# Eight adaptive rows as matrix products of a broadcast column with raw weight tiles, in a three-layer transformer kernel

## The chip, the cores and the metric

The kernel runs on one core of one Trainium2 chip. The metric is the device time of one execution in microseconds (us), the median of several runs. The engines are named as in the profile: PE (TensorE, with PEld for its weight loads), DVE (VectorE), ACT (ScalarE), POOL (GpSimd) and SP (SyncE, whose queue issues most loads). Each engine works through its own instructions in the order in which they stand.

## The reference, cut to what matters

The program is a hybrid layer (attention with a learned choice of keys, a short convolution, a mixture of 64 experts) and two more transformer layers behind it, on 512 tokens of 1024 features. The change touches one vector of the first layer:

```python
ada = jax.nn.silu(c) @ w_ada + b_ada            # [1, 6 * 1024]
shift1, scale1, gate1, shift2, scale2, gate2 = [a[:, None, :] for a in jnp.split(ada, 6, axis=-1)]
h = rms_norm(x, norm1_g) * (1 + scale1) + shift1
proj = h @ w_in                                  # conv inputs, q, k, v, index q, index k, index weights
score = relu(qi . ki) weighted by wi             # the 128 best keys of each query are kept
x = x + gate1 * mix
h2 = rms_norm(x, norm2_g) * (1 + scale2) + shift2
x = x + gate2 * moe(h2, ...)
```

`w_ada` is 1024 x 6144, 24 MB in float32. Its 6144 columns are handled in twelve groups of 512, numbered 0 to 11. Groups 2, 0, 3 and 1 (scale1 and shift1) are needed before the first projection; the other eight, in the order 8, 9, 6, 7, 4, 5, 10, 11, are needed only after attention. They are the "late rows".

## The kernel before, in words

Each matrix product is made from two exact parts of both operands (`split`, L217 on ACT and L218 on DVE or POOL, makes them; `mm3`, L225 to L227, makes three products). Weights come through `_Stream`: SP loads 1 MB raw tiles (`wraw`) ahead, in the order of `plan_attn`, and the tiles of `w_ada` are used raw. All eight PSUM banks belong to one pool (`ps()`), and most large SBUF tiles to another.

`attn_block` does, in this order on PE: the early ada rows and the normalised, transposed tokens (until 62.5 us); the second half of the index queries (`first(wb, ...)`, four chunks of 12 products); the index keys (`psk`, 24 products); then `proj` for k, for q and for v. Each `proj` holds four accumulators, one per token tile `tt`, and goes through eight chunks `kc` of 12 products (four token tiles by three). After each chunk `tick()` emits one step of each piece of background work: `heads_T` (normalises k or q on DVE, L478 to L492 and the rotation L420 to L423, transposes on PE, L230, and splits, L220 and L221), `topk` (index scores on PE, L725 on ACT and L728 to L737 on DVE, then 16 rounds of L748 and L752 on DVE, ending in the mask `selbias`, L756) and `aw`, the late rows. Twenty steps of the convolution follow, then attention, whose first product of each query tile reads `selbias` (L816).

A late row has four steps of `aw`. In a step ACT scales two 128 x 512 slices of the raw tile by a column of silu(c) (L655) and POOL adds them up (L657). Two rows later `ada_sum` makes one product of a matrix of ones with the sum (L605), which adds over the partitions and puts the result on all of them, and DVE adds it to the row (L608, L609 or L611). `ada_feed`, called where `proj` takes a weight tile, takes the two raw tiles of the next row and issues the loads of bias and gain on ACT's queue when its count reaches NR, NR + 1 and NF.

The early rows (`ada`, L545) are already made in the other way: `cb` holds silu(c) with each value repeated along 128 columns, and eight float32 products of `cb` with a raw slice give the row on all partitions.

Of the kernel before, what the change touches and what calls it, by code (L numbers as in the profile page):

```python
# [23 lines left out]
NT = 4  # L24
# [9 lines left out]
# slots of an expert by its rank: those below the first number have the second  # L34
# [3 lines left out]
NR=3; RQ=3; RV=2  # L38
NF=7
BU=1  # L40
ADA='aaaaaaaa'
# [29 lines left out]
class _Stream:  # L71
    """Weights in the order of use: loads run ahead on the SP queue, and each tile is split into two
    parts of at most 12 significant bits, whose sum is the float32 value, before it is used."""
# [57 lines left out]
    def more(self):  # L131
        """prepare one more tile than `ahead` asks for"""
        if self.ns < len(self.jobs):
            if self.ns not in self.rawt:
                self.pump(self.ns)
            self._split()
            self.pump(self.ns)
# [40 lines left out]
class _K:  # L178
# [53 lines left out]
    def rsqrt(self, v, n, scale, eps, name):  # L232
        """1 / sqrt(scale v + eps): a seed from the exponent, a third-order step and a Newton step, each on a
        multiple of the result that spares a product"""
# [42 lines left out]
    def tick(self):  # L277
        """emit one step of each piece of background work"""
        self.todo[:] = [g for g in self.todo if next(g, self) is not self]
# [5 lines left out]
    def proj(self, hT, nk, tiles, n=512, hook=None, w=None):  # L285
        """token-major product: weight tiles [p, kk, n] from chunk kc0 on into four PSUM tiles"""
# [14 lines left out]
    def by_tile(self, part, done, early=()):  # L301
        """products that end tile by tile: done(tt, *part(tt)) goes on by a step once the next tile's products
        are emitted; the functions `early` come after the last tile's products, a step of `done` apart"""
# [16 lines left out]
    def part(self, hT, ps, tt, ws):  # L320
        """token tile tt of a product, weight tiles [(first chunk, tile)]"""
# [7 lines left out]
    def begin(self, xT):  # L329
        """the products of a block's first two weight tiles [128, 8, 256] with the first half of the tokens"""  # L330
# [16 lines left out]
    def begun(self, xT):  # L347
        """what `begin` has left of the next of its weight tiles"""
        w, ps = self.head.pop(0)
        self.cols(xT, w, ps, slice(256, 512))  # L350
        return ps

    def chunks(self, name, n):
        """feature-major operand in chunks of 128 features by 512 columns, as its two exact parts"""
# [58 lines left out]
    def rope_p(self, t, cc, ss):  # L413
        """rotate the first 16 of each 64 columns of t [128, G, 64]; cc [128,16], ss [128,16] = [-sin | sin]"""
# [50 lines left out]
    def row(self, dst, ap, off, n):  # L465
        """one DRAM row on all partitions"""
        self.nc.scalar.dma_start(out=dst, in_=bass.AP(tensor=ap.tensor, offset=ap.offset + off, ap=[[0, 128], [1, n]]))

    def heads_T(self, dst, ps, g=None, scale=None):
        """four PSUM tiles [128 tok, 8 x 64]: (RMS norm with gain g,) partial rotation, feature-major split;  # L470
        the gain of the rotated columns goes in before the rotation, that of the others, in `scale`, after it"""
# [33 lines left out]
    def attn_block(self):  # L505
        nc, V, a, st = self.nc, self.nc.vector, self.a, self.st
        # adaptive scale and shift, and the normalised tokens, by halves of the features
# [86 lines left out]
        # remaining adaptive rows, on the scalar and Pool engines  # L594
# [4 lines left out]
        wait = []  # L599

        def ada_sum():
            n, t = wait.pop(0)
            ps = self.ps()
            c = slice((n % 4) * 512, (n % 4) * 512 + 512)
            nc.tensor.matmul(ps, ones, t, start=True, stop=True)  # L605
# [22 lines left out]
        def ada_work():  # L628
            for i, n in enumerate(todo):
                while not fed:  # L630
                    yield
                ws = fed.pop(0)
                if len(wait) > 1:
                    ada_sum()
                t = self.sm([128, 512], "p", bufs=3)
                col = lambda j, kk: cs[:, 4 * j + kk:4 * j + kk + 1]
                if ADA[i] == "d":
                    for j in range(2):
                        for kk in range(4):
                            x, c = ws[j][:, kk], col(j, kk)  # L640
                            if j + kk:
                                V.scalar_tensor_tensor(t, x, c, t, op0=OP.mult, op1=OP.add)
                            else:
                                V.tensor_scalar(t, x, c, None, OP.mult)
                            if kk % 2:
                                yield
                else:
                    ts = self.slot(F32, "adap")
                    for j in range(2):
                        for kk in range(4):  # L650
                            x = ts[:, kk * 512:kk * 512 + 512]
                            if ADA[i] == "p" or ADA[i] == "h" and kk % 2:
                                nc.gpsimd.tensor_scalar(x, ws[j][:, kk], col(j, kk), None, OP.mult)
                            else:
                                nc.scalar.activation(x, ws[j][:, kk], AF.Copy, scale=col(j, kk))  # L655
                            if j + kk:
                                nc.gpsimd.tensor_tensor(out=t, in0=x if j or kk > 1 else ts[:, :512], in1=t if j or kk > 1 else x, op=OP.add)  # L657
                            if kk % 2:
                                yield
                wait.append((n, t))  # L660
            yield self
        aw = ada_work()
        # indexer queries, keys, weights
# [43 lines left out]
        # indexer scores  # L707
# [31 lines left out]
        def topk():  # L739
            """the 128 best keys of each query, the earlier of equal ones: others get a bias of -1e30"""  # L740
# [23 lines left out]
        # values  # L764
# [5 lines left out]
        # short convolution, channel-major  # L770
# [34 lines left out]
        while wait:  # L805
            ada_sum()
        # attention
# [41 lines left out]
        # the rest of the output projection and the residual, then the normalised tokens of the expert half  # L849
# [29 lines left out]
    def out_head(self, mix, add):  # L879
        """the first four chunks' share of an output projection; add(tt, ps, n) takes it in"""  # L880
# [22 lines left out]
    def pipeline(self, items, stages, fill=None, n=0, ready=None):  # L903
        """stages [(fn, delay)] over items; each step also emits up to n units of the background work `fill`,
        and as much of it as an item needs to be ready"""
# [24 lines left out]
    def attend(self, heads, logits, value, fill=None, n=0, bufs=3, ready=None):  # L930
        """softmax attention of `heads` in tiles of 128 queries, feature-major result"""
# [34 lines left out]
    def moe_units(self):  # L966
        """(ranks, rows of the slot blocks), in the order of work: the first FIX experts; the others by falling
        number of tokens, the busiest with two blocks, the least busy two to a block"""
# [50 lines left out]
    def moe_begin(self, hT):  # L1019
        """the router and most of the shared expert's first products, on the first half of the tokens"""  # L1020
# [66 lines left out]
    def moe_block(self, hT, h2d, x1d):  # L1087
# [20 lines left out]
        pos_b = self.const.tile([128, NT, NE], BF16, name="pos_b")  # exact up to 256, and above stays above  # L1108
# [10 lines left out]
        def pack(v, g, tmp):  # L1119
            """the gate in three exact parts"""  # L1120
# [8 lines left out]
        def tables(c, ig, is_):  # L1129
            """gather and scatter rows of n blocks from the sums c [128, n, 3] of token, tile base and one"""  # L1130
# [1015 lines left out]
```

## Time and profile before

| what | value |
|---|---|
| median of three runs | 2726.62 us |
| lowest and highest of them | 2722.79 and 2729.9 us |
| span of the profiled execution | 2724.9 us |
| mean granted clock of PE in it | 0.938 of full speed |
| PE busy in the span | 2361.5 us, 87% |
| DVE, ACT, POOL busy | 1649.5, 1056.4, 836.8 us |

The profile gives no time of that execution apart from its span, so the span stands for both; it lies 1.7 us under the median. Averages over the span say little about the change, which touches only the stretch from 62 to 260 us.

### The profile page before, as it was taken

What the parts mean: (1) busy time and instruction counts of PE and PEld (TensorE: products, weight loads), DVE (VectorE), ACT (ScalarE), POOL (GpSimd) and SP (SyncE); (2) the same over time, 40 slices, a digit from 0 to 9 for tenths busy, and PEclk for the clock granted to TensorE, in tenths of its full rate; (3) what the DMA queues carried; (4) which work ended last, traced back from release to release, by engine and by line L of the source; (5) the groups of instructions that cost most, each with busy time, mean ns of one, the idle gap of its engine ahead of it and who ended that gap; (6) DMA issues with size and microseconds to landing.
All of it is one profiled execution on the core that took longest, in us unless ns stands there. A gap on an engine that the chain in (4) does not pass through costs nothing.

```text
span 2724.9 us, 33197 instructions
## 1 busy us (share of the span) xinstructions
PE 2361.5 (87%) x12964; PEld 1979.8 (73%) x12964; DVE 1649.5 (61%) x2445; ACT 1056.4 (39%) x1446; POOL 836.8 (31%) x308
## 2 busy tenths in 40 slices
PE   8778996778777887888758998999999998899998
PEld 4556765677666776777757877888888886788887
DVE  4699666577877877677656655333354666533234
ACT  2642433355545655555542532221313443222221
POOL 0653243456645655565521120000032221100001
PEclk9889998899988988898979999999999998999999
DMA  9432145588967877888861042223232122222321
GB/s 317 171 122 63 47 157 188 192 264 273 308 212 245 287 260 248 278 278 279 271 182 45 16 152 88 85 93 108 87 114 70 47 72 81 95 89 81 123 70 39
DMA packets 176593, 422.40 MB, mean 155 GB/s; under 512 B 19281, under 2 KB 97873, under 8 KB 151729
## 3 DMA queue, kind: packets, MB, share of 16 engines
q1 hardware_dynamic: 151552, 353.43, 37.8%
q0 software_dynamic: 12944, 39.20, 6.7%
q10 hardware_dynamic: 11938, 27.62, 2.8%
q8 instruction: 103, 1.69, 0.2%
q14 instruction: 56, 0.46, 0.1%
HBM read 390.78 MB, written 35.52 MB: 156 GB/s over the span
## 4 chain that ended last, share of the span: by engine, by line
PE 50%; DVE 22%; issue 9%; DMA 7%; ACT 6%; POOL 6%; ACTq 0%; POOLq 0%; DVEq 0%; SPq 0%
PE b L225 16%; PE b L226 15%; PE b L227 15%; DVE wl L218 5%; POOL wl L218 4%; ACT wh L217 4%; DMA acc<-eo,isc 3%; PE b L230 2%; DMA wraw<-in_w_dram 2%; DVE xet L218 1%; DVE gt L1140 1%; DVE work L752 1%; DVE eo L1414 1%; PE b L545 1%; POOL acc L1218 1%
## 5 line engine op out<-in xcount | busy, mean ns | idle before, releaser
L218 POOL TENSOR_TENSOR wl<-wraw,wh 128x2048 fp32r<-128x2048 f32 (+2 forms) x113 | 533.0, 4720 | 1208.6 <-ACT wh L217 1157.8
L218 DVE TENSOR_TENSOR wl<-wraw,wh 128x2048 fp32r<-128x2048 f32 x198 | 606.9, 3072 | 367.8 <-ACT wh L217 319.6
L217 ACT ACTIVATE wh<-wraw 128x2048 fp32r<-128x2048 f32 (+2 forms) x311 | 583.5, 1884 | 151.3 <-DVE wl L218 58.0
L225 PE MATMUL b<-xtl,wh 128*128 128x512 f32 (+1 forms) x928 | 342.5, 369 | 2.9 <-DVE xtl L218 2.9
L226 PE MATMUL b<-xth,wl 128*128 128x512 f32 (+1 forms) x928 | 341.0, 368 | 4.0 <-POOL wl L218 4.0
L227 PE MATMUL b<-xth,wh 128*128 128x512 f32 (+1 forms) x928 | 340.7, 367 | 0.0
L225 PE MATMUL b<-wl,xet 128*128 128x256 f32 x1072 | 319.2, 298 | 0.1
L226 PE MATMUL b<-wh,xet 128*128 128x256 f32 x1072 | 311.3, 290 | 0.8 <-DVE xet L218 0.8
L227 PE MATMUL b<-wh,xet 128*128 128x256 f32 x1072 | 310.8, 290 | 0.0
L1218 POOL DMA_INDIRECT acc<-eo,isc x67 | 102.6, 1531 | 391.9 <-DVE P L1152 121.6
L225 PEld LDWEIGHTS b<-wl,xet 128*128 128x128 f32 x1072 | 214.7, 200 | 1.7 <-ACT xet L217 0.2
L226 PEld LDWEIGHTS b<-wh,xet 128*128 128x128 f32 x1072 | 214.0, 200 | 2.4 <-DVE xet L218 0.9
L227 PEld LDWEIGHTS b<-wh,xet 128*128 128x128 f32 x1072 | 213.2, 199 | 0.0
L225 PE MATMUL b<-wl,aet 128*128 128x512 f32 x268 | 125.5, 468 | 99.6 <-POOL wl L218 99.1
L226 PEld LDWEIGHTS b<-xth,wl 128*128 128x128 f32 x928 | 175.0, 189 | 32.8 <-POOL wl L218 4.6
L225 PEld LDWEIGHTS b<-xtl,wh 128*128 128x128 f32 x928 | 175.0, 189 | 32.3 <-DVE xtl L218 3.6
L227 PEld LDWEIGHTS b<-xth,wh 128*128 128x128 f32 x928 | 174.9, 189 | 28.9
L225 PEld LDWEIGHTS b<-wl,aet 128*128 128x128 f32 x268 | 57.8, 216 | 121.2 <-POOL wl L218 108.8
L225 PE MATMUL b<-wl,ath 128*128 128x512 f32 x352 | 137.1, 390 | 0.0
L227 PE MATMUL b<-wh,ath 128*128 128x512 f32 x352 | 136.9, 389 | 0.0
L226 PE MATMUL b<-wh,atl 128*128 128x512 f32 x352 | 136.9, 389 | 0.0
L1213 POOL DMA_INDIRECT xg<-h2d,ig x51 | 124.6, 2444 | 34.3 <-issue 17.5
(463 smaller groups left out, 4649.8 us busy)
## 6 DMA issues: line engine op xcount, KB each, us to landing
wraw<-in_w_dram SPq DMA_DIRECT2D x192, 1024.0 KB
wraw<-in_ffn_w_gu_dram SPq DMA_DIRECT2D x44, 1024.0 KB
wraw<-in_w_ada_dram SPq DMA_DIRECT2D x24, 1024.0 KB
wraw<-in_ffn_w_down_dram SPq DMA_DIRECT2D x20, 1024.0 KB
wraw<-in_diff_w_in_dram SPq DMA_DIRECT2D x12, 1024.0 KB
wraw<-in_w_in_dram SPq DMA_DIRECT2D x8, 1024.0 KB
wraw<-in_w_in_dram SPq DMA_DIRECT2D x12, 512.0 KB
x<-in_x_dram SPq DMA_DIRECT2D x8, 512.0 KB
```

The lines of the kernel that those rows point to most:

```text
L217: nc.scalar.activation(H, x, AF.Copy)
L218: (eng or nc.vector).tensor_tensor(out=L, in0=x, in1=H.bitcast(F32), op=OP.subtract)
L225: mm(ps, s[0], m[1], start=start, stop=False)
L226: mm(ps, s[1], m[0], start=False, stop=False)
L227: mm(ps, s[0], m[0], start=False, stop=stop)
L230: self.nc.tensor.transpose(ps, x, self.ident[:x.shape[0], :x.shape[0]])
L545: nc.tensor.matmul(ps, cb[:, kc, :], w[:, kk, :], start=False, stop=kc == 7)
L752: V.match_replace(work(qt), m8[qt - 1], work(qt), -3e38)
L1140: V.tensor_tensor(out=gt, in0=c[:, :, 2], in1=c[:, :, 1], op=OP.add)
L1213: nc.gpsimd.indirect_dma_start(out=x, out_offset=None, in_=h2d, in_offset=IndirectOffsetOnAxis(ap=idx, axis=0), bounds_check=S - 1, oob_is ...
L1218: nc.gpsimd.indirect_dma_start(out=acc, out_offset=IndirectOffsetOnAxis(ap=idx, axis=0), in_=o, in_offset=None, compute_op=OP.add)
L1414: V.tensor_scalar(o[rows, c], ps[rows], gate[rows], None, OP.mult)
```

## The change

The late rows are made as the early ones are. A step of `aw` is now two float32 products on PE, `cb` with two raw slices, summed in a PSUM bank that the row holds through its four steps. `ada_sum`, the ACT scalings, the POOL sums, their tiles `adap` and `p` and the products with ones are gone. The DVE sum with the bias (`ada_row`) stands right after the row's last step and no longer two rows later. NR goes from 3 to 1, so that the loads of gain and bias are issued with the first and second row. (Comments and docstrings are gone too.)

```diff
-NR=3; RQ=3; RV=2
+NR=1; RQ=3; RV=2
...
-        wait = []
-
-        def ada_sum():
-            n, t = wait.pop(0)
-            ps = self.ps()
+        def ada_row(n, ps):
             c = slice((n % 4) * 512, (n % 4) * 512 + 512)
-            nc.tensor.matmul(ps, ones, t, start=True, stop=True)
             r = rows[(n - 4) // 4][:, c]
...
         def ada_work():
-            for i, n in enumerate(todo):
+            for n in todo:
                 while not fed:
                     yield
                 ws = fed.pop(0)
-                if len(wait) > 1:
-                    ada_sum()
-                t = self.sm([128, 512], "p", bufs=3)
-                col = lambda j, kk: cs[:, 4 * j + kk:4 * j + kk + 1]
...
-                    ts = self.slot(F32, "adap")
-                    for j in range(2):
-                        for kk in range(4):
-                            x = ts[:, kk * 512:kk * 512 + 512]
...
-                                nc.scalar.activation(x, ws[j][:, kk], AF.Copy, scale=col(j, kk))
-                            if j + kk:
-                                nc.gpsimd.tensor_tensor(out=t, in0=x if j or kk > 1 else ts[:, :512], in1=t if j or kk > 1 else x, op=OP.add)
-                            if kk % 2:
-                                yield
-                wait.append((n, t))
+                ps = self.ps()
+                for j in range(2):
+                    for kk in range(4):
+                        kc = 4 * j + kk
+                        nc.tensor.matmul(ps, cb[:, kc, :], ws[j][:, kk, :], start=kc == 0, stop=kc == 7)
+                        if kk % 2:
+                            yield
+                ada_row(n, ps)
...
         self.drain()
-        while wait:
-            ada_sum()
```

On PE, at the head of the projection for q, these rows stood before: the product with ones (out of `p`), then the first chunk's products of three of the four token tiles, with the engines that each waits for.

```order
L605 MATMUL b<-p,ones_f 128x512 [waits Activation_49,Pool_49]
L225 MATMUL b<-wl,hth 128x512 [waits Activation_49]
L226 MATMUL b<-wh,htl 128x512
L227 MATMUL b<-wh,hth 128x512
...
L225 MATMUL b<-wl,hth 128x512 [waits DVE_49]
L226 MATMUL b<-wh,htl 128x512
```

In the changed kernel (its line numbers are lower by one or more) the same place reads so; `g_98` is the tile that holds `cb`, and L633 is the new product.

```order
L633 MATMUL b<-wraw,g_98 128x512 [waits DMAHW4_49,Activation_49]
L633 MATMUL b<-wraw,g_98 128x512
L224 MATMUL b<-wl,hth 128x512 [waits Activation_49]
...
L224 MATMUL b<-wl,hth 128x512 [waits DVE_49]
L225 MATMUL b<-wh,htl 128x512
L226 MATMUL b<-wh,hth 128x512
L224 MATMUL b<-wl,hth 128x512 [waits DVE_49,Activation_49]
L225 MATMUL b<-wh,htl 128x512
L226 MATMUL b<-wh,hth 128x512
L633 MATMUL b<-wraw,g_98 128x512 x2
L224 MATMUL b<-wl,hth 128x512
```

A pair of new products now stands ahead of every chunk of k, q and v, and two token tiles of the first chunk wait for DVE where one did. The built program gives the fourth token tile of q the bank of k's first accumulator, so its wait is for the DVE multiply that reads that accumulator last (L490, L489 in the changed kernel); before, it had the bank of the ones product and waited for the row's sum (L611). At the head of v it is the same with q's first accumulator.

On DVE, at the start of the stretch, these rows stood before: the split of the index-key weights, those of both tiles of k's weights, and the first row's sum and gain.

```order
L218 TENSOR_TENSOR wl<-wraw,wh 128x576
L218 TENSOR_TENSOR wl<-wraw,wh 128x2048 x2
L608 SCALAR_TENSOR_TENSOR row_417<-b,row_417 128x512
L609 TENSOR_TENSOR row_417<-row_417 128x512
L420 TENSOR_TENSOR rpa_590<-t2k,rope_c 128x128
```

Now they stand so:

```order
L217 TENSOR_TENSOR wl<-wraw,wh 128x576
L603 SCALAR_TENSOR_TENSOR row_417<-b,row_417 128x512
L604 TENSOR_TENSOR row_417<-row_417 128x512
L217 TENSOR_TENSOR wl<-wraw,wh 128x2048
L603 SCALAR_TENSOR_TENSOR row_417<-b,row_417 128x512
```

The sums of the first two rows moved ahead of the splits of k's two weight tiles.

## Rows read from the trace of the kernel before

**Rows 1.** The page's first line, the whole execution.

```profile
span 2724.9 us, 33197 instructions
```

**Rows 2.** Windows: stretch, length, busy time of PE, PEld, DVE, ACT, POOL; clock.

```profile
62.50:126.90 64.40, 53.35 (x223) 38.48 (x221) 37.96 (x79) 35.78 (x56) 41.41 (x28) 0.87 0.48 165
126.90:141.80 14.90, 11.31 (x40) 8.16 (x38) 14.16 (x20) 8.91 (x15) 8.45 (x6) 0.89 0.61 210
141.80:172.90 31.10, 24.39 (x126) 18.41 (x127) 27.53 (x45) 15.87 (x29) 16.29 (x10) 0.89 0.20 68
172.90:191.80 18.90, 8.21 (x23) 5.98 (x24) 18.07 (x34) 8.34 (x14) 11.14 (x7) 0.64 0.63 195
191.80:256.90 65.10, 53.38 (x230) 41.56 (x228) 64.55 (x171) 17.41 (x22) 25.36 (x12) 0.97 0.33 82
```

**Rows 3.** Waits of PE, 62.5 to 257 us: total, times, longest.

```profile
PE b L225 <- DVE row L611: 19.0, 3, 10.7
PE b L230 <- DVE t2k L700: 5.4, 4, 3.9
PE b L225 <- ACT t2k L679: 2.7, 1, 2.7
PE b L225 <- ACT t2k L495: 2.5, 1, 2.5
```

**Rows 4.** Chain that ended last: eight raw products, then one split product; start, us.

```profile
48.53 7.06 PE b L545 x16
55.83 0.23 PE b L226
```

**Rows 5.** Instructions of the tile adap, its readers among them: duration min/median/max.

```profile
L655 ACT ACTIVATE adap<-wraw,cs x64: 703/712/775, 66.3 to 217.2; 128x512 f32<-128x512 f32 x64
L657 POOL TENSOR_TENSOR p<-adap,p x48: 1262/1294/3225, 69.1 to 220.3; 128x512 f32<-128x512 f32 x48
```

**Rows 6.** Instructions of L492, L730 and L736 on DVE: min/median/max in ns.

```profile
L492 DVE TENSOR_TENSOR t2k<-t2k,q_norm_g x4: 292/554/4317, 191.8 to 211.2; 128x128 f32<-128x128 f32 x4
L730 DVE SCALAR_TENSOR_TENSOR work<-t2k,kwt,work x21: 484/750/1652, 123.1 to 175.3; 128x512 f32<-128x512 f32 x7, 128x384 f32<-128x384 f32 x7, 128x256 f32<-128x256 f32 x7
L736 DVE TENSOR_SCALAR work<-work x3: 417/1323/4628, 157.4 to 175.9; 128x512 f32<-128x512 f32 x1, 128x384 f32<-128x384 f32 x1, 128x256 f32<-128x256 f32 x1
```

**Rows 7.** Timeline of DVE, and one row of POOL: start, us, engine.

```profile
135.93 1.24 DVE L237 TENSOR_SCALAR rs_t<-hn_ss 128x32 f32<-128x32 f32 x1
141.12 0.69 DVE L490 TENSOR_TENSOR t2k<-b,hn_r 128x512 f32<-128x512 f32 x1
149.63 4.55 POOL L218 TENSOR_TENSOR wl<-wraw,wh 128x2048 fp32r<-128x2048 f32 x1 [1.67 <-ACT wh L217]
150.00 4.33 DVE L492 TENSOR_TENSOR t2k<-t2k,k_norm_g 128x128 f32<-128x128 f32 x1
189.10 0.18 DVE L237 TENSOR_SCALAR rs_t<-hn_ss 128x32 f32<-128x32 f32 x1
191.11 0.69 DVE L490 TENSOR_TENSOR t2k<-b,hn_r 128x512 f32<-128x512 f32 x1
256.53 0.90 DVE L756 TENSOR_SCALAR selbias<-work 128x256 fp32r<-128x256 f32 x3
257.94 1.28 DVE L611 TENSOR_TENSOR row<-row,b 128x512 f32<-128x512 f32 x2
```

**Rows 8.** Timeline of PE at the seams: start, us, idle before and releaser.

```profile
60.90 1.91 PE L230 MATMUL b<-ident,x 128*128 128x128 f32 x16
126.61 0.40 PE L227 MATMUL b<-kit,qith 64*128 64x512 f32 x2
133.58 0.74 PE L225 MATMUL b<-wl,hth 128*128 128x512 f32 x1 [3.31 <-DVE row L611]
172.44 0.28 PE L227 MATMUL b<-kit,qith 64*128 64x256 f32 x2
186.75 0.79 PE L225 MATMUL b<-wl,hth 128*128 128x512 f32 x1 [10.66 <-DVE row L611]
```

More of the change, by code (lines that the diff above doesn't have):

```diff
@@ L37 @@
 MORE=(5,6)
-NR=3; RQ=3; RV=2
+NR=1; RQ=3; RV=2
 NF=7
 BU=1
-ADA='aaaaaaaa'
 TC=3; TY=(1, 0, 0)
@@ L632, in ada_work @@
                 ws = fed.pop(0)
-                if len(wait) > 1:
-                    ada_sum()
-                t = self.sm([128, 512], "p", bufs=3)
-                col = lambda j, kk: cs[:, 4 * j + kk:4 * j + kk + 1]
-                if ADA[i] == "d":
-                    for j in range(2):
-                        for kk in range(4):
-                            x, c = ws[j][:, kk], col(j, kk)
-                            if j + kk:
-                                V.scalar_tensor_tensor(t, x, c, t, op0=OP.mult, op1=OP.add)
-                            else:
-                                V.tensor_scalar(t, x, c, None, OP.mult)
-                            if kk % 2:
-                                yield
-                else:
-                    ts = self.slot(F32, "adap")
-                    for j in range(2):
-                        for kk in range(4):
-                            x = ts[:, kk * 512:kk * 512 + 512]
-                            if ADA[i] == "p" or ADA[i] == "h" and kk % 2:
-                                nc.gpsimd.tensor_scalar(x, ws[j][:, kk], col(j, kk), None, OP.mult)
-                            else:
-                                nc.scalar.activation(x, ws[j][:, kk], AF.Copy, scale=col(j, kk))
-                            if j + kk:
-                                nc.gpsimd.tensor_tensor(out=t, in0=x if j or kk > 1 else ts[:, :512], in1=t if j or kk > 1 else x, op=OP.add)
-                            if kk % 2:
-                                yield
-                wait.append((n, t))
+                ps = self.ps()
[6 more added lines that the diff above has]
+                ada_row(n, ps)
             yield self
```

## The prediction, made before the changed kernel ran

> **What bounds the kernel now.** I read the page first: one execution spans 2724.9 us [rows 1], 1.7 under the median 2726.6, so the sum is made against the span and 1.7 is added at the end. The late rows lie between the last early transposes (PE, to 62.5) and the mask of the first attention tile (DVE, from 256.5, ready about 0.3 later). The windows of that stretch [rows 2] show who is full where. Until 126.9 PE is busy for 53.4 of 64.4 us; after that DVE is full (14.2 of 14.9, 27.5 of 31.1, 18.1 of 18.9, 64.6 of 65.1) and PE stands idle for parts. Over all five windows PE is busy 150.6 of 194.4 us, so 43.8 us are free, and its clock is below full. The waits [rows 3] say what PE waits for: 19.0 us for DVE row sums (L611), which stand behind DVE's index scores and rounds, 5.4 for index keys (L700), 5.2 for ACT copies that free banks (L679 and L495). So the stretch is a DVE chain that PE feeds: the scores of PE start DVE's rounds, and the normalisation on DVE gives PE back its banks.
>
> **The change, part by part.**
>
> *Price.* Eight raw products took 7.06 us at full clock, 0.88 each; a split product takes 0.23 [rows 4]. A pair costs 1.765. There are 32 pairs: 56.5 us on PE. The eight products with ones (the same shape, 0.88 each) go: 7.0. Net 49.4 us more PE work, against 43.8 us of idle time in the stretch. Off ACT go 64 x 0.712 = 45.6 us, off POOL 56 x about 1.29 = 72 us [rows 5]. Neither engine is the one waited for at the end of a window, so this counts only where it held DVE or PE. I put it in below.
>
> *A, 62.5 to the last index scores of 512 keys (126.9).* PE does 168 split products of 0.23 (48 index queries, 24 index keys, 96 for k), 38.6 us, score products 2.8, transposes 2.5 (my counts, each 0.45 per four) and two ones products 1.8: 45.7 us of work in 64.4. The rest is waiting and half clock. The waits for L679, L495 and L700 [rows 3] go away: ACT is free when the bank is to be emptied, and the DVE chain for the index keys starts earlier against a slower PE. 16 pairs come in: 45.7 - 1.8 + 28.2 = 72.1, so this point comes at 134.6, **+7.7**. The loads of gain and bias, now issued near 67 us, have 10 us before row 8 is done; I cost them at nothing. If they were late, k's splits on DVE would be too, with 10 us in hand.
>
> *B, from there to DVE's first L490 of k.* Before, 126.9 to 141.8. The chain from L237 to L490 took 5.2 us (135.93 to 141.12), and the same chain for q 2.0 (189.10 to 191.11), when POOL had no sums to make [rows 7]. So 3.2 us go: 11.7, which ends at 146.3, **+4.5** against before. Here is the new wait. The fourth token tile of q's first chunk used to wait for the row sum (L611, until 133.58 [rows 8]); it now waits for this L490, as its bank is k's first accumulator, the new row having taken a bank for four chunks. Queued behind it on PE is all the rest of q. PE, done with what it can do at 138.5, stands for 8 us.
>
> *C, from there to the last scores (before, 172.6 [rows 8]).* PE has 3 + 84 split products, 20.0 us, seven pairs, 12.4, scores and transposes, 5.3, and starts at half clock (before, after such a wait, the window's clock was 0.64 [rows 2] and PE lost half of some 3 us): 1.6. The split of v's first weight tile on POOL starts 2 us after the second k tile is back, as before, and then the two-input DVE instruction L492 took 4.33 instead of 0.29 us, to the end of POOL's 4.55 us [rows 6, 7]; this holds the row sum and so the scores by 3.5. Sum 42.8, to 189.1, **+16.5**. This is where most of the work lands: before, PE came to this point with 11 us of waits.
>
> *D, from the last scores to DVE's first L490 of q.* Before, 172.6 to 191.1 plus 0.7: 19.2. L736 was held by a POOL split, 4.63 us where its shortest is 0.42 [rows 6], so 4.2; the last seven L730 ran near the median of 0.750 where the minimum is 0.484, 1.9 [rows 6]; and the instruction behind L736 was held by most of one POOL sum of 1.29 [rows 5], 0.9. That is 7.0. In the changed order DVE reaches L736 about 1 us before POOL's split starts. 19.2 - 7.0 = 12.2, to 201.3, **+9.5** against 191.8. PE waits for it with v's fourth token tile; before, it waited only for the row sum (186.75 [rows 8]).
>
> *E, from there to selbias (256.5).* Before 64.7 us, all DVE. POOL's sums held three instructions, each by at most one of 1.29 [rows 5], 2.5 in all: these go. One more row sum falls in: +0.7. DVE has to wait for q's transposes, since a chunk on PE now takes 4.5 instead of 2.7 us: the first is back 12 us after the seam, and DVE has 9 us of work ahead of it, the later ones cost 1 more; +4.3. The convolution's first split on POOL still holds L492 (4.3 us, in the 64.7 already). 64.7 - 2.5 + 0.7 + 4.3 = 67.2, to 268.5, **+12.0**. PE alone would be there sooner: three products, 84 more, seven pairs, 1.8 of transposes, 27.3 for 120 convolution products, 1.6 of clock: 63 us.
>
> *After it.* The two row sums at 257.94 (1.28 us [rows 7]), ahead of attention's first reductions on DVE, are gone: **-1.3**. Nothing else moves; SP's loads stand in the same order, and the raw tiles of the last row are asked for when the last scores are done and used four chunks (18 us) later, so they cost nothing. I take the shift as carried to the end one to one, since the order behind it is unchanged.
>
> **Sum:** 12.0 - 1.3 = +10.7, 2735.6 on the span, **2737** on the median. The bounds of the unknown: the two POOL holds (in C and E) turn on tenths of a microsecond between ACT's split and DVE's L492. Without them C and E lose 3.5 and 4.0: +3.3, 2730. With a third (L736 in D, as before) it is +15, 2742.
>
> **A rule weighed against this.** The row for L492 shows 0.29 us alone and 4.33 beside a POOL split that ends when it ends [rows 6, 7]. The Trainium skill, GPSIMD Engine Reference, section "8. Key points", says that GpSimd shares its SBUF interfaces with VectorE and that they contend where the VectorE instruction has two SBUF inputs or a two-port mode; the trace agrees. By it every POOL sum taken away gives DVE time back, which speaks for the first rival.
>
> **Rivals.**
>
> 1. *Faster: DVE sets the end throughout, and PE's work fills its idle time.* DVE gets back what the POOL sums held: 3.2 in B, up to 21 x (0.750 - 0.484) = 5.6 in L730 [rows 6, 7], the 1.3 at the end, and 4.2 at L736: -14, **2712**. For it: DVE is full after 126.9 [rows 2], and 43.8 us of PE idle time nearly hold the 49.4. Against it: the idle time is idle because PE waits for DVE, and DVE's scores start when PE's products allow. It wins if the last scores come before 177, which needs PE to lose under 5 us in A to C. Chance 0.13.
>
> 2. *No change.* The same sum without the POOL holds, 2730, or with the shift partly absorbed by a later wait for weights or a scatter: **2730**. For it: the holds are a matter of tenths. Chance 0.40.
>
> 3. *Much slower: the bank held by the row stops PE at both seams, and little of the idle time is used.* If half of the 43.8 us stays idle, 49.4 - 21.9 = +27.5, less 3.2: **2751**. It decides if PE stands over 12 us at each seam. Chance 0.12.
>
> The forecast, slower by the sum above, 2733 to 2743, has 0.35.
>
> **How the numbers follow.** A measurement of this kernel tells about 0.3%, 8.2 us, from no change: 2718.4 to 2734.8 is the same. Faster is rival 1, 0.13. The same is rival 2 and a little of the forecast's low end, 0.43. Slower is the rest of the forecast and rival 3, 0.44. The range for 8 in 10 goes from inside rival 1 to rival 3: 2715 to 2750.
>
> **What would show it.** In the changed profile: 64 new raw products of L633 near 0.88 us, no wait for L679 or L700, the last 512-key score near 134.6, a PE wait of 7 to 9 us for the multiply L489 near 139 to 146 and one of about 10 us before 201, the last scores near 189, selbias near 268. ACT and POOL should be less busy by 46 and 72 us. The prediction is wrong if selbias comes before 256 (rival 1), if L492 is never held (rival 2), or if the stretch behind 268 does not keep the shift.

## The result, and the profile after

The changed kernel takes 2751.06 us (median), the kernel before, on the same chip, 2728.26: **1.0087 times as long, 95% interval 1.0073 to 1.0101**, or 22.8 us more. The forecast was slower by 10.7. The direction was right; the size was less than half of it, and 2751.06 lies 1.1 us above the range of 2715 to 2750.

The first lines of the changed kernel's page give the span and the busy time of each engine.

```profile
span 2750.2 us, 33232 instructions
PE 2411.0 (88%) x13076; PEld 2002.0 (73%) x13076; DVE 1622.5 (59%) x2445; ACT 1016.3 (37%) x1382; POOL 755.4 (27%) x252
```

PE is 49.5 us busier (its line of the page before has 2361.5), where the prediction had 49.4. This count also holds products that ran at half speed, so that it agrees so closely is in part luck; but the price of a pair, read below, was right too, and is not what went wrong. The windows of the changed kernel, cut at the same five events as [rows 2] (the end of the early transposes, the last 512-key scores, the first multiply of k, the last scores, the first multiply of q, the selection mask), show where the time went. The columns are those of [rows 2].

```profile
65.20:140.40 75.20, 74.40 (x280) 47.75 (x280) 29.18 (x82) 16.48 (x24) 0.00 (x0) 1.00 0.45 158
140.40:150.80 10.40, 4.08 (x14) 2.34 (x13) 9.81 (x20) 4.39 (x7) 0.00 (x0) 0.92 0.51 177
150.80:201.70 50.90, 46.66 (x180) 30.61 (x180) 22.37 (x45) 10.40 (x20) 4.57 (x1) 0.88 0.19 62
201.70:214.10 12.40, 5.01 (x14) 2.62 (x13) 11.76 (x32) 4.13 (x6) 4.54 (x1) 0.72 0.95 286
214.10:282.20 68.10, 64.83 (x262) 48.10 (x262) 63.16 (x171) 11.27 (x12) 13.81 (x3) 0.98 0.32 80
```

The lengths add up to 217.0 us; those of [rows 2] to 194.4. The difference, 22.6, is nearly the 22.8 that was timed; from the mask to the end both profiles take 2468.4 us. (The early transposes stand at 60.9 in the profile before and at 63.3 in this one. They lie between 58.3 and 63.3 in the profiles of all kernels here, whatever was edited, so stretches are counted from there on. The part behind the mask takes 2462 to 2479 us in these profiles, one execution of each kernel, so single microseconds of it can't be read off a pair of spans.) PE is now full in the first stretch, at full clock (1.00 in its row); DVE, which was busy for 27.5 of 31.1 us in the third window before, has 28.5 us of idle time there.

Set against the forecast, with two of the experiments below (lengths in us, from the windows; the forecast's fifth ends at the mask itself, 0.4 sooner):

| stretch | before | forecast | after | rows in one step | the same, splits on DVE |
|---|---|---|---|---|---|
| A, to the last 512-key scores | 64.4 | 72.1 | 75.2 | 72.0 | 72.0 |
| B, to the first multiply of k | 14.9 | 11.7 | 10.4 | 10.7 | 10.6 |
| C, to the last scores | 31.1 | 42.8 | 50.9 | 44.7 | 41.0 |
| D, to the first multiply of q | 18.9 | 12.2 | 12.4 | 12.5 | 14.7 |
| E, to the mask | 65.1 | 67.2 | 68.1 | 67.6 | 64.3 |

Stretch C is 8.1 us longer than forecast, A 3.1; the others are within 1.3. What PE waits for in the changed kernel, 62.5 to 282 us (total, times, longest), answers to [rows 3]:

```profile
PE b L224 <- DVE t2k L489: 10.0, 2, 6.4
PE b L224 <- DVE row L606: 6.7, 2, 4.0
PE b L224 <- ACT t2k L701: 1.2, 2, 0.6
PE b L633 <- ACT t2k L494: 0.7, 1, 0.7
```

The waits for L700 and L679 are gone, and all waits of PE ahead of the mask come to 18.6 us, where those shown in [rows 3] alone came to 29.6; but PE carries 49 us more. Three things in PE's timeline were not in the sum. First the chunks of the first stretch, which behave as forecast, then a group of four heads' 512-key scores:

```profile
69.86 1.88 PE L633 MATMUL b<-wraw,g 128*128 128x512 f32 x4
74.34 1.88 PE L633 MATMUL b<-wraw,g 128*128 128x512 f32 x4
130.64 0.50 PE L224 MATMUL b<-kit,qith 64*128 64x512 f32 x2
130.97 0.40 PE L225 MATMUL b<-kit,qitl 64*128 64x512 f32 x2
131.21 0.40 PE L226 MATMUL b<-kit,qith 64*128 64x512 f32 x2
131.44 0.39 PE L224 MATMUL b<-kit,qith 64*128 64x512 f32 x1
131.68 0.38 PE L225 MATMUL b<-kit,qitl 64*128 64x512 f32 x1
131.90 0.39 PE L226 MATMUL b<-kit,qith 64*128 64x512 f32 x1
132.29 0.49 PE L224 MATMUL b<-kit,qith 64*128 64x512 f32 x1
132.62 0.39 PE L225 MATMUL b<-kit,qitl 64*128 64x512 f32 x1
132.86 0.39 PE L226 MATMUL b<-kit,qith 64*128 64x512 f32 x1
133.18 1.12 PE L633 MATMUL b<-wraw,g 128*128 128x512 f32 x2
```

A chunk with a pair takes 74.34 - 69.86 = 4.48 us; twelve split products of 0.23 are 2.77 of it, so a pair costs 1.71 (forecast 1.765). The scores are the surprise. A head's products use 64 rows of the array, and two heads run side by side: "x2" is two products that start together. Here only the first two heads do; the third runs alone, and the fourth starts when an ACT copy (L701) has emptied the first head's bank, since four accumulators and the open row leave three banks. The group takes 2.6 us (130.64 to 133.25). In the kernel before, a group of four heads with 512 keys ran all in pairs and took 1.65 us.

The first seam, the held row sum and the clock, from the timelines of PE, POOL and DVE:

```profile
150.88 0.76 PE L224 MATMUL b<-wl,hth 128*128 128x512 f32 x1 [6.40 <-DVE t2k L489]
152.29 3.61 PE L633 MATMUL b<-wraw,g 128*128 128x512 f32 x4
158.54 1.88 PE L633 MATMUL b<-wraw,g 128*128 128x512 f32 x4
171.12 4.57 POOL L217 TENSOR_TENSOR wl<-wraw,wh 128x2048 fp32r<-128x2048 f32 x1 [169.83 <-ACT wh L216]
171.19 4.59 DVE L420 TENSOR_TENSOR rpb<-t2k,rope_s 128x64 f32<-128x64 f32 x1
175.70 0.21 DVE L421 TENSOR_TENSOR rpb<-t2k,rope_s 128x64 f32<-128x64 f32 x1
176.16 0.68 DVE L606 TENSOR_TENSOR row<-row,b 128x512 f32<-128x512 f32 x1
176.89 0.70 PE L224 MATMUL b<-kit,qith 64*128 64x384 f32 x2 [2.74 <-DVE row L606]
180.10 3.50 PE L633 MATMUL b<-wraw,g 128*128 128x512 f32 x4
```

After the stop of 6.40 us PE's products run at half speed (a pair 3.61 in place of 1.88); the second stop, of 2.74 us, is followed by the same (3.50). The granted clock is 0.51 of full speed from 150.8 to 156.0 and 0.53 from 176.8 to 183.6, and 1.00 from 156 to 176: the lower and the upper of its two levels. That second stop is the row's bank again: the score product needs it, the row sum L606 empties it, and L606 stands on DVE behind L420, which POOL's split holds for 4.59 us. (The kernel before had such a stop of a score product too, 5.07 us, one of the three for L611 in [rows 3].)

### The profile page after: what moved, and what is told of

It reads as the page before. It is cut to its first block, busy times and chain, and to the rows that moved or that the text cites. A ratio compares the mean times of both kernels' runs of the same rounds, so it can differ in the third digit from the quotient of the medians.

```text
span 2750.2 us, 33232 instructions
## 1 busy us (share of the span) xinstructions
PE 2411.0 (88%) x13076; PEld 2002.0 (73%) x13076; DVE 1622.5 (59%) x2445; ACT 1016.3 (37%) x1382; POOL 755.4 (27%) x252
## 4 chain that ended last, share of the span: by engine, by line
PE 53%; DVE 19%; issue 9%; DMA 7%; ACT 6%; POOL 6%; ACTq 0%; POOLq 0%; SPq 0%; DVEq 0%
PE b L224 16%; PE b L225 15%; PE b L226 15%; DVE wl L217 5%; POOL wl L217 5%; ACT wh L216 4%; DMA acc<-eo,isc 3%; PE b L229 2%; PE b L633 2%; DMA wraw<-in_w_dram 2%; DVE xet L217 1%; DVE gt L1114 1%; POOL acc L1192 1%; DVE eo L1388 1%; PE b L544 1%
```

## Experiments

Two theories. **P**: the price of the pairs on a full PE is the loss. **B**: on top of the price, the PSUM bank that an open row holds costs time at the scores and seams. **H** is a part by itself: POOL's splits hold DVE.

**The rows by stretch.** Rows of one stretch from products on PE, the others by ACT and POOL as before. (NR is 1, as in the change, in the first of these runs, and 3, as before, in the other two.)

```
 for n in todo:
     ...
     if n in PE_ROWS:   # (8, 9, 6, 7), (4, 5) or (10, 11)
         ...            # eight products, as in the change
     else:
         ...            # ACT scalings, POOL sums, ones product, as before
```

> Rows 8, 9, 6 and 7 come from products on PE as in the change, rows 4, 5, 10 and 11 from ACT scalings, POOL sums and a ones product as before. Theory P (the price of the pairs on a full PE is the loss): PE stays full from the early transposes to the last 512-key scores, 16 pairs of 1.71 us, so this point comes 8 to 12 us later than before and 5 to 10 us of that reach the end: ratio 1.002 to 1.004. Theory B (the bank that a row holds over the seams is the loss): no row product holds a bank at either seam here, so at most 1.002, within 4 us of before.

> Only rows 4 and 5 (fed with q's chunks) come from products on PE. Theory P: 8 pairs, 13.7 us, between the first seam and the last scores, where PE was on the path with 11 us of waits before; with half-clock time after the seam, +5 to +9 us: 1.002 to 1.0033. Theory B: the wait for the first multiply L489 of k's heads shows up at q's fourth token tile and is the greater part, 6 us or more, of a loss of 8 us or more: 1.003 or over.

> Only rows 10 and 11 (fed with v's chunks) come from products on PE. Theory P: behind the last scores DVE sets the time and PE has idle time, so the pairs are hidden: -3 to +3 us, 0.999 to 1.001. Theory B: the bank held at v's seam stops PE for 5 us or more, which reaches the selection mask: +5 us or more, 1.002 or over.

Measured: rows 8, 9, 6, 7: **1.0035** (1.002 to 1.0051); rows 4, 5: **1.0030** (1.0018 to 1.0042); rows 10, 11: **1.0014** (1.0003 to 1.0025). Of 2729 us these are 9.6, 8.2 and 3.8 us, 21.6 together: the loss is spread over all three stretches and nearly adds up to the whole. The first run's time is P's; but its rows hold a bank over the two groups of 512-key scores, and these groups are broken there as in the changed kernel, while its groups of 256 keys, where no row is open, run in pairs. So it speaks against a loss at the seams alone, and not against the bank. The second run's time fits both, though its wait for k's first multiply is 3.56 us and not the 6 that B asked for; the third lies between. The waits for that multiply (L490 in these kernels) behind a seam appear in the two runs whose rows span that seam, and only there: 3.56 us each.

**A quarter of the products.**

```
-    nc.tensor.matmul(ps, cb[:, kc, :], ws[j][:, kk, :], start=kc == 0, stop=kc == 7)
+    if kc in (0, 7):
+        nc.tensor.matmul(ps, cb[:, kc, :], ws[j][:, kk, :], start=kc == 0, stop=kc == 7)
```

> The change with only the first and last of the eight products of each row (the rows are not the right sums): every bank, wait, load and row sum stays, three quarters of the PE price (41 of 54.7 us) go. Theory P: the last 512-key scores come at 120 to 128, the last scores before 177, and the whole is faster than before by what the POOL sums and ACT scalings cost, 0.994 to 0.998 of before. Theory B: the waits at the seams stay, and with them most of the loss: 1.003 or over.

Measured: **0.9957** (0.9946 to 0.9969). Without most of the price the changed kernel beats the one before by 11.8 us: the work taken off ACT and POOL is worth something, and the price eats it. This is P's side: 41 us of products less gave back 35 us. The score groups stay broken and the seam wait is there (6.45 us), so this run does not clear B of a part; but B's 1.003 or over fails here, and with it the reading that the waits at the seams are most of the loss.

**The bank: a row in one step.** All eight products in the third of the row's four chunks; same products, the bank held for one step.

```
-    ps = self.ps()
-    for j in range(2):
-        for kk in range(4):
...
-            if kk % 2:
-                yield
-    ada_row(n, ps)
+    for step in range(4):
+        if step == 2:
+            ps = self.ps()
+            for kc in range(8):
+                nc.tensor.matmul(ps, cb[:, kc, :], ws[kc // 4][:, kc % 4, :], ...)
+            ada_row(n, ps)
+        yield
```

> The change with the eight products of a row in one step (the third of its four chunks) in place of four steps of two: the same 56 us of products, but no row holds a PSUM bank over the index scores of other chunks or over a seam. Theory P (the price alone): at most 3 us back, ratio to before 1.007 or over. Theory B (the held bank on top of the price: the fourth score product of a group waits for an ACT copy, 1.06 us for each of eight groups, and the stop of 6.4 us at the seam with 2.3 us of half clock behind it): 8 to 12 us of the 23 back, 1.004 to 1.0055; groups of four 512-key scores take 1.5 us in place of 2.5, and PE waits under 3 us for L489 at the first seam.

Measured: **1.0068** (1.0047 to 1.0088), which overlaps the changed kernel's interval. That is 5 us back, short of the 8 to 12 that B asked for and over the 3 that P allowed, so the time alone does not decide. The windows speak for B, 207.5 us in place of 217.0, but the part behind the mask is 3.6 us longer in this profile. Its windows A and C, and then, from PE's timeline, a score group and the first seam:

```profile
60.40:132.40 72.00, 72.00 (x282) 46.66 (x280) 29.05 (x82) 15.57 (x23) 0.00 (x0) 1.00 0.47 163
143.10:187.80 44.70, 43.29 (x168) 27.04 (x168) 22.52 (x45) 9.49 (x19) 4.60 (x1) 0.91 0.22 71
```

```profile
126.20 0.50 PE L224 MATMUL b<-kit,qith 64*128 64x512 f32 x2
126.54 0.40 PE L225 MATMUL b<-kit,qitl 64*128 64x512 f32 x2
126.77 0.40 PE L226 MATMUL b<-kit,qith 64*128 64x512 f32 x2
127.01 0.40 PE L224 MATMUL b<-kit,qith 64*128 64x512 f32 x2
127.24 0.39 PE L225 MATMUL b<-kit,qitl 64*128 64x512 f32 x2
127.47 0.40 PE L226 MATMUL b<-kit,qith 64*128 64x512 f32 x2
143.15 2.90 PE L633 MATMUL b<-wraw,g 128*128 128x512 f32 x3 [5.02 <-issue]
```

All four heads run in pairs, in 1.7 us (126.20 to 127.87) against 2.6; my 1.5 was a little low, and there are six such groups (two of 512, two of 384, two of 256 keys), not the eight of the expectation. The groups of 256 keys run in pairs too. The two of 384 keys do not, though no row is open there; the second of them did not in the kernel before either. Both stand right behind a group of transposes (L229); that these hold the missing bank is not shown. The Trainium skill, "TensorE: Matmul & The Clock Gate", section "Why this matters for your kernels", says that products with few rows run concurrently when they lie in distinct row groups; the trace agrees while each has a free bank, and shows that a held bank takes this away. PE still stops for 5.02 us at the seam, where 3 at most was expected, but two chunks of q later, so less is left behind the stop. (The profile names no releaser; the stop ends 0.1 us after the first multiply of k, L489, from 142.36 to 143.05.) The eight products take 7.03 us in one go where PE is at full clock, as in [rows 4].

The same edit with a quarter of the products isolates the bank from the price:

```
     if step == 2:
         ...
-        for kc in range(8):
+        for kc in (0, 7):
```

> The change with only the first and last of the eight products of each row (the rows are not the right sums), both in one step, the third of the row's four chunks. Against the run with the same two products four chunks apart (0.9957 of before) only the time for which a row holds its PSUM bank differs. Theory B: 3 to 7 us less, 0.993 to 0.9948, the groups of four 512-key scores at 1.5 us, and no wait of 6 us for L489 behind the first seam. If the bank costs nothing without the price: 0.995 to 0.997.

Measured: **0.9898** (0.9872 to 0.9925) against 0.9957 (0.9946 to 0.9969): the intervals are apart. The longer hold costs 16 us (0.0059 of 2729; from the intervals some 8 to 24), more than twice what B allowed. The windows of C, first the four-step run, then the one-step run, show most of it:

```profile
129.00:171.20 42.20, 37.11 (x158) 27.45 (x159) 22.44 (x46) 10.41 (x21) 4.54 (x1) 0.87 0.14 50
```

```profile
124.10:156.20 32.10, 30.70 (x144) 21.69 (x144) 22.42 (x45) 9.45 (x19) 4.59 (x1) 0.94 0.29 99
```

Ten of the 16 us lie here, and 14.3 in the five windows together. A part of the ten is work that PE could do ahead of its stop: 72 split products of q are left in the one-step window and 87 in the other, 3.5 us at 0.23 each. POOL's split is there in both (4.5 us), and only where the row is open does PE stop for its row sum (3.58 us in the first, no such wait in the second). The edit also moves the times at which the raw tiles are read, but PE waits for no load in either profile of this stretch, and DVE for one of about the same length in both (7.8 and 7.1 us, for a bias).

**POOL's splits.** The low parts of v's two tiles and of the convolution's first pair are split on DVE, in the changed kernel, in the one-step kernel, and in the kernel before.

```
-        first += [(w, "pool") for w, _ in self.plan_win(2560)]
+        first += self.plan_win(2560)
...
-        j += [(cols[i:i + 2], "pool") for i in range(0, 12, 2)]
+        j += [(cols[i:i + 2], True if i < 2 else "pool") for i in range(0, 12, 2)]
```

> The change with the low part of v's two weight tiles and of the convolution's first pair split on DVE (2.3 us each) in place of POOL (4.6 us). Theory H (POOL's split holds the DVE instruction beside it, L420 for 4.59 us, twice, with a wait of 2.7 us of PE and half clock of 2.9 us behind the first): no L420 over 0.3 us, 4 to 8 us of the 23 back, 1.0055 to 1.007. Rival: DVE has idle time in its place, and pays 2.3 us for each split where it has none: 1.008 to 1.010.

> Both edits: the rows in one step each, and the three splits on DVE. If B and H hold and are separate, 12 to 18 of the 23 us back: 1.002 to 1.004. If the price alone is the loss, 1.007 or over. If the two remove the same wait, no more back than by the better of the two.

> The kernel before with the low parts of v's two tiles and of the convolution's first pair split on DVE in place of POOL, and nothing else. Theory H: as with rows 8 and 9 on DVE, 5 to 8 us, 0.997 to 0.998. Rival: the two edits need each other, 0.9985 or over.

Measured: in the changed kernel **1.0076** (1.0059 to 1.0093), no gain that the timing can tell; with one step **1.0045** (1.0028 to 1.0062), apart from the changed kernel and a little short of the 1.002 to 1.004 expected; in the kernel before **0.9975** (0.9962 to 0.9987), a gain of 6.8 us. In the first of them the mask does come 6.0 us sooner after the early transposes (275.62 - 63.06 against 281.84 - 63.25), but the next split on POOL holds a DVE instruction behind the mask, and now PE waits for the softmax. DVE, then PE, of that run:

```profile
275.62 0.90 DVE L732 TENSOR_SCALAR selbias<-work 128x256 fp32r<-128x256 f32 x3
280.38 4.90 DVE L771 SCALAR_TENSOR_TENSOR t2k<-t2k,cw 128x510 f32<-128x510 f32 x1
286.55 0.48 PE L229 MATMUL b<-ident,p 128*128 128x128 f32 x1 [4.47 <-DVE p L920]
```

The changed kernel has the same hold, but there PE waits 3.14 us for the mask, runs at a granted clock of 0.50 for the next 9.8 us and is busy for all of them; here it waits 0.99, runs at 0.94 and is through with its work sooner. So a part of what H gives is taken back at once; how much of the rest is real in the changed kernel, the timing leaves open.

**What is left when both are mended.** The one-step kernel with the splits, and a quarter of the products in rows 8, 9, 6 and 7 only:

```
-                            nc.tensor.matmul(ps, ...)
+                            if n in (4, 5, 10, 11) or kc in (0, 7):
+                                nc.tensor.matmul(ps, ...)
```

> The run with one step a row and the splits on DVE (1.0045 of before), with only the first and last of the eight products in rows 8, 9, 6 and 7 (these rows are not the right sums): 20.5 us less on PE in the stretch up to the last 512-key scores. Theory P: the whole of what is left of the loss goes, and 2 us or more besides: 0.997 to 1.0005; the scores come 57 to 62 us after the early transposes, in place of 73.5. Rival (what is left lies behind the first seam): 1.002 or over.

Measured: **0.9949** (0.9932 to 0.9967), 26 us less than the run with all products, for 20.5 us less of products. The last 512-key scores come 54.4 us after the early transposes (113.96 - 59.55), sooner than the 57 to 62 expected. That is 19.1 us sooner than the 73.5 of the run with all products, close to the 20.5 taken out: in stretch A, where PE is full, the price is paid one to one. The timing gives back more than P allowed (0.997 at best); where the rest of the 26 us lies is not shown.

**Rows on DVE, and which rows PE can take.** Rows 8 and 9 as multiply-adds on DVE, in the kernel before; then with other rows from products in one step (letters for rows 8, 9, 6, 7, 4, 5, 10, 11: d on DVE, a by ACT and POOL, m products on PE; NR is 2 in the run with six m, 3 in the others).

```
-ADA='aaaaaaaa'
+ADA='ddaaaaaa'   # then 'ddmmmmmm' with the three splits, 'ddaaaamm', 'ddaaaaam'
```

> The kernel before with rows 8 and 9 summed on DVE (eight multiply-adds of 0.75 us a row) in place of 16 ACT scalings and 14 POOL sums; the ones products stay. Tests what the removal of ACT and POOL work in the first stretch is worth without a price on PE. Theory A (ACT's copies L679 and L495 stand behind scalings, and PE waits for them): these waits, 5.2 us, go, 0.998 to 0.999. Rival: 12 us more on DVE delay the index-key chain that ends in L700 by as much or more: 1.0 to 1.003.

> Rows 8 and 9 summed on DVE with a ones product, the other six from products on PE in one step each, the three splits of v and the convolution on DVE: the run with both edits, with half of the price taken off PE in the first stretch (13.7 us, 1.8 of ones products back). Theory P (what is left of the loss, 8 to 11 us, is the price in the stretch up to the last 512-key scores, where PE is full): this point comes 6 to 10 us earlier after the early transposes than the 73.5 us of that run, ratio 1.000 to 1.002. Rival (the loss left is in the later two stretches): 1.003 or over.

> The kernel before with rows 8 and 9 on DVE, and rows 10 and 11 from products on PE in one step each; rows 6, 7, 4 and 5 by ACT and POOL. Theory P with the bank (behind the last scores DVE sets the time; PE's idle time takes two rows if none holds a bank over the seam): as the run with rows 8 and 9 on DVE or better, 0.996 to 0.9985. Rival (13.7 us more on PE make it the one that ends last before the selection mask, whatever the steps): 1.0 or over.

> As the last one with only row 11 from products on PE: half the price behind the last scores, one of the two row sums ahead of attention gone. Theory P: 0.9965 to 0.9985. Rival (PE bound there): 0.9985 to 1.0, half of what the two rows cost.

Measured: rows 8 and 9 on DVE **0.9984** (0.9972 to 0.9996): within theory A's bounds; the wait for L679 is gone and that for L495 is 1.3 us in place of 2.5, but PE waits 3.9 us anew for the first row's sum. With six rows on PE **1.0027** (1.0017 to 1.0038), a miss: the scores come only 3.6 us earlier, since PE now waits for a row sum that stands on DVE behind the multiply-adds and a split, the row shown; the time lies between P's range and the rival's. With two late rows on PE **1.0000** (0.9991 to 1.0009), with one **0.9996** (0.9984 to 1.0007): the rivals held, no gain over 0.9984.

```profile
88.15 0.79 PE L225 MATMUL b<-wl,hth 128*128 128x512 f32 x1 [6.32 <-DVE row L611]
```

With two late rows PE waits 1.06 us for the mask, where it waited 5.6 before: 13.7 us of products fill its idle time up to the brim, and gain nothing.

**The fastest version** has rows 8 and 9 on DVE and the three splits; one more split taken off POOL makes it slower again.

```
-ADA='aaaaaaaa'
+ADA='ddaaaaaa'
...
+        first += self.plan_win(2560)
+        j += [(cols[i:i + 2], True if i < 2 else "pool") for i in range(0, 12, 2)]   # then i < 4
```

> The kernel before with rows 8 and 9 on DVE and with the low parts of v's two tiles and of the convolution's first pair split on DVE in place of POOL. Theory H (each POOL split holds one DVE instruction to its end, some 4 us, and costs DVE 2.3 us when it does it itself): 2 to 6 us better than rows 8 and 9 on DVE alone, 0.9962 to 0.998. Rival (DVE is full from the first seam to the selection mask, and pays 6.9 us for what it gets back): 0.9985 to 1.001.

> The kernel before with rows 8 and 9 on DVE, and v's two and the convolution's first two splits on DVE in place of POOL. Against three splits (0.9961) the split that holds the multiply-add of the convolution for 4.9 us behind the selection mask is gone, and with it the delay of the first softmax: 2 to 4 us more, 0.9945 to 0.9955. Rival: DVE is full there and PE's half clock and conv products cover the delay: 0.9958 to 0.997.

Measured: **0.9961** (0.9947 to 0.9975), 10.6 us faster than before and faster than the changed kernel by over 1%, as the two edits alone add up to (0.9984 and 0.9975). With the fourth split on DVE **0.9987** (0.9977 to 0.9998), slower than either theory allowed: in its profile DVE's own split comes late for the convolution, and PE waits for it:

```profile
222.42 0.80 PE L226 MATMUL b<-hth,wl 128*128 128x512 f32 x1 [6.73 <-DVE wl L218]
```

## Why the prediction was right in direction and short in size

- **What bounds the kernel** was read rightly: a chain of DVE work that PE feeds, with 43.8 us of PE's idle time in it. Rival 1 (DVE sets the end, PE's work fills the idle time) fails: the quarter run shows that the gain it counted exists (0.9957), but only without the price. (Its 5.6 us for L730 takes the shortest of three shapes for all 21; in the changed kernel those of 512, 384 and 256 keys take 0.75, 0.62 and 0.48 us.)
- **Price**: right. 1.71 us a pair against 1.765; 32 of them less the ones products are 47.7 us against 49.4, and the 49.5 of the page holds half-speed time besides. ACT is 40.1 us less busy (1056.4 before) for 46, POOL 81.4 (836.8 before) for 72.
- **Step A**, +7.7: the sum of 72.1 us is what the one-step kernel takes, 72.0. The changed kernel takes 75.2. Of its 3.1 us more the two broken score groups are 1.8 (0.9 each) and a wait for L494 is 0.74; the bank held by the row was put at nothing here. The removed waits and the loads of gain and bias came as forecast.
- **Step B**, +4.5: the chain to the first multiply took 10.4 against 11.7, and the new wait of PE for L489 at q's fourth token tile is there, 6.4 us for 8.
- **Step C is the step that failed**: 42.8 us forecast, 50.9 measured. Its 87 split products and some seven pairs are those of the sum; the rest was mis-sized, mostly since the sum let the scores run as if no row held a bank. Scores and transposes at 5.3 assumed that heads run in pairs, and the hold by POOL's split was 3.5; from the rows below, the four groups of scores take 6.7, 2.4, 1.6 and 1.7 us, waits of 3.9 in them, and with 1.9 of transposes that is 14.3 where the sum had 8.8. (The second of these groups, the 2.4, took 2.1 us in the kernel before too, so little of its excess is the row's.) POOL's split held L420 (and not L492) for 4.59 us, and reached PE through the row's bank. The half clock was charged once, 1.6; it came twice, as the pairs of 3.61 and 3.50 us against 1.88 show, and cost about 4.1 outside the scores (my estimate, from the starts of these products and of the same at full clock). These two, 5.5 and 2.5, are the 8.1 us.

```profile
173.37 0.44 PE L224 MATMUL b<-kit,qith 64*128 64x384 f32 x1
186.71 0.45 PE L224 MATMUL b<-kit,qith 64*128 64x384 f32 x2
189.06 1.98 PE L633 MATMUL b<-wraw,g 128*128 128x512 f32 x4
193.74 0.39 PE L224 MATMUL b<-kit,qith 64*128 64x256 f32 x2
195.37 1.98 PE L633 MATMUL b<-wraw,g 128*128 128x512 f32 x4
200.05 0.39 PE L224 MATMUL b<-kit,qith 64*128 64x256 f32 x2
201.48 0.27 PE L226 MATMUL b<-kit,qith 64*128 64x256 f32 x1
```

  In the one-step kernel, where the row's bank is free in time, this step takes 44.7, and without the splits on POOL 41.0. These lie around the 42.8, but they do not prove its sum: 15 of the 87 split products are done ahead of the step there, and it has eight pairs.
- **Step D**, 12.2, measured 12.4. **Step E**, 67.2, measured 68.1: DVE waits 4.4 us for q's transposes (forecast 4.3), and POOL's split holds it there too, on L420 at 233.6.
- **After it, -1.3**: absent. In place of the two row sums DVE waits for an ACT copy, and the multiply-add behind it ends with POOL's split, as one did before (L795, 4.92 us); from the mask to attention's first reduction both kernels take 9.6 us:

```profile
281.84 0.90 DVE L732 TENSOR_SCALAR selbias<-work 128x256 fp32r<-128x256 f32 x3
284.58 0.69 DVE L768 TENSOR_TENSOR t2k<-t2k,b 128x512 f32<-128x512 f32 x1 [1.24 <-ACT t2k L766]
286.61 4.92 DVE L771 SCALAR_TENSOR_TENSOR t2k<-t2k,cw 128x510 f32<-128x510 f32 x1
```

- **The rivals.** The time is that of rival 3, 2751. Its sum took half of PE's 43.8 us of idle time, 21.9, to stay idle, and PE is idle for 22.0 of the 217.0 us; but PE did not stand over 12 us at each seam, only 6.4 us at the first and 4.0 and 3.6 at the second. Its cause, the bank held by the row, was right, but in part in the wrong place: I charged the bank at the seams only, and not at the scores between them.

So the missing 12 us are 3.1 in A, 8.1 in C and 1.3 behind the mask; B, D and E together come to -0.6. That holding a row's bank for four chunks costs time of this order is shown by the quarter runs, where one edit, all of a row's products in one step, takes the 16 us away. With all products the one-step kernel gives back 9.5 us in its windows and 5 by its timing, which overlaps the changed kernel's; how much of the missing 12 us the bank is in the changed kernel itself stays open. The shares of broken pairs, half clock and row-sum wait within it are read from the timeline and were not tried one by one.

## What to carry to other kernels

An accumulator that stays open over other work costs a PSUM bank for all that time: count, at each point in between, how many banks the other work rotates through, and what it loses with one less; all products of a row in one step cost the same on PE and hold the bank for one step in place of four. Work moved onto the engine that feeds the critical chain is paid in full wherever that engine is full, and idle time counted over a long stretch says nothing on where. A milestone that comes sooner is no gain by itself: where the next hold stands right behind it, only the time of the whole tells.

## What the runs showed of the hardware

A DVE instruction of 128x64 elements, 0.22 us alone, took 4.59 us when POOL's split started 0.07 us before it: it ended with the split, however small it was. The convolution's multiply-add, 0.75 us alone, took 4.92. This is its duration in the instructions of L771 of the changed kernel (minimum, median, maximum in ns):

```profile
L771 DVE SCALAR_TENSOR_TENSOR t2k<-t2k,cw x2: 749/2833/4917, 279.5 to 286.6; 128x510 f32<-128x510 f32 x2
```

The Trainium skill, "SBUF — State Buffer", section "Summary: rules for kernel authors", says that a VectorE instruction with two SBUF inputs and a GpSimd instruction that reads SBUF do not overlap, and that the second to issue waits for the first; the trace agrees. Here the whole split of 4.6 us has to be charged to whichever two-input DVE instruction comes next, and moving three such splits to DVE, which needs 2.3 us for each, made the kernel before 6.8 us faster.
